# A hybrid diffusion block: full-height filter products, and adaLN products on two column tiles

## The chip, the core and the metric

The kernel runs on one core of a Trainium2 chip. The metric is the time of one execution in microseconds of the device; lower is better. Engines are named as in the profile: PE (TensorE matmuls), PEld (TensorE weight loads), DVE (VectorE), ACT (ScalarE), POOL (GpSimd) and SP (SyncE, which issues most transfers).

## The reference, cut to what matters

One layer of a diffusion backbone over 512 latent tokens and 256 context tokens of width 1024. An adaLN vector (`silu(c) @ w_mod + b_mod`, for the latent and for the context condition) gives shifts and scales; the normed and modulated tokens go through one input projection into three mixers (a gated DeltaNet, a Hyena long convolution, an RG-LRU recurrence); their gated sum is projected and added; then comes a gated ConvFFN.

The change touches two things that are computed before the first projection. The first is the Hyena filter:

```python
hid = jnp.sin(f2 * (hid @ w2 + b2))            # (512, 64)
filt = (hid @ w3).reshape(n, 2, HY_WIDTH)      # two filters of 1024 channels
filt = filt * jnp.exp(-t * deltas)[:, None, :]
```

whose Fourier spectrum multiplies the sequence later. The second is the first third of the adaLN product, the shift and scale of norm 1: a product of the two condition vectors (1024 long) with a 1024 x 2048 part of `w_mod`.

## The kernel before, in words

All matmuls that need single precision are either float32 matmuls (each shows as two LDWEIGHTS and two MATMUL records) or sums of float32r products of a high and a low part (one record each). Everything of interest is the opening stage, before the first input projection. Its order is written out by hand: the string `ORDER` is a list of steps, each a letter and a number, and every engine and SP's queue keeps its instructions in the order of that list. Steps that matter:

- `M`: load 512 KB of `w_mod` (16 of them, M0 to M15), into a ring of six 4 KB buffers; `D`: load decay factors; `x`: load 1/8 of the tokens; `s`: store a spectrum; `L`: load and split a projection weight.
- `m` (`mod_mm`, lines 378 to 383): unit u multiplies the 128 x 32 condition tile (two columns used) with both 512-column halves of buffer u, into two PSUM banks, both at partitions 0 to 31. Units 10, 11 and 13 are split first by the steps `p10`, `p11` and `P13` (`mod_split`, lines 370 to 375: one ACT copy, two subtractions on DVE or POOL) and multiplied as two float32r products.
- `a`, `A` (`filt`, line 320): filter u, eight matmuls with 256 columns. They alternate between a product of all 128 rows (the high parts of `w3` against `hid2`, which holds the high part of the hidden layer in rows 0 to 63 and the low part in rows 64 to 127) and one of 64 rows (the low part of `w3`, line 331). DVE multiplies each result by the decay (line 333), ACT and DVE or POOL split it (lines 155 and 160).
- `b`, `B` (`spectrum`): 24 products of 128 rows and 256 columns (lines 173 to 175), then DVE, ACT and POOL work on the results (lines 347 to 362).
- `q`, `Q`, `N`, `O`, `n`, `y`: sums of squares, the norm, and the scaling of the tokens by it (lines 399 to 420). `V`: split `w3` on ACT and POOL (line 455).
- `T`, `E` (`mod_T`, `mod_out`): transposes of the adaLN results out of PSUM (line 389), then scale and shift. `h` (`h_out`): modulate one eighth of the tokens on ACT, POOL and DVE (lines 437 to 439); the first input projection needs all eight.

On PE the order is: l0 m0 l1 m1 m2 a0 m3 A1 m4 m5 B0 A2 m6 m7 A3 m8 b1 b2 A4 b3 N B4 O m9 m10 m11 m12 A5 A6 a7 m13 m14 m15 b5 b6 b7, then the first projection. PSUM results of filters and spectra share four banks (`dn`).

Of the kernel before, what the change touches and what calls it, by code (L numbers as in the profile page):

```python
# [10 lines left out]
F32 = mybir.dt.float32  # L11
F32R = mybir.dt.float32r
AF = mybir.ActivationFunctionType
ALU = mybir.AluOpType
# [3 lines left out]
P = 128  # L18
D = 1024
# [3 lines left out]
KD = D // P  # L23
# [38 lines left out]
def seq(off, kb, n):  # L62
    return [off + kb * i for i in range(n)]
# [2 lines left out]
ARENA = 196  # L66


ORDER = """W l0 U0 M D x1 u1 m0 M x4 x2 M M x3 M x0 f0 V1 V0 l1 m1 m2 M f1 Q0 a0 D m3 M A1 q1 m4 m5 Q2 B0 M A2 x5 q3 M D m6 m7 q4 T0 x6 I q5 M A3 m8 b1 x7 Q6 b2 Q7 A4 b3 N K L0 M p10 s1 M p11 B4 O n4 M m9 m10 m11 m12 T1 D M s2 y7 n1 s3 M y0 P13 s4 n3 y5 n2 A5 A6 a7 M m13 m14 m15 E y6 b5 h0 h1 b6 h2 h3 s0 b7 h4 h5 L1 h6 h7 s5 s6 s7"""
FBT = (1, 4)  # L70


# [1 line left out]
def tile_block(ctx: ExitStack, tc: tile.TileContext, I: dict, out: bass.AP, dbg=None, upto=99):  # L74
    nc = tc.nc
# [7 lines left out]
    def shaped(ap, shape):  # L83
        shape = list(shape)
        if len(shape) == 2:
            return ap
        names = "abcde"[:len(shape) - 1]
        return ap.rearrange("p (%s) -> p %s" % (" ".join(names), " ".join(names)),
                            **{n: d for n, d in zip(names[1:], shape[2:])})

    def at(off, shape, dt=F32, kb=None):

        n = int(np.prod(shape[1:]))
        size = int(kb * 256) if kb else n
        assert n <= size and off * 256 + size <= ARENA * 256, (shape, off, kb)
        key = (off, size, dt)
        if key not in regions:
            regions[key] = nc.alloc_sbuf_tensor_at(f"region{len(regions)}", [P, size], dt, offset=base + int(off * 1024)).ap()
        return shaped(regions[key][0:shape[0], 0:n], shape)

    def ring(kb, offs):
        return Ring(at, kb, offs)
# [11 lines left out]
    def c1(shape, name, dt=F32):  # L114
        return sb.tile(shape, dt, tag=name, bufs=1, name=name)
# [9 lines left out]
    act = nc.scalar.activation  # L125
    stt = nc.vector.scalar_tensor_tensor
    vtt = nc.vector.tensor_tensor
    gtt = nc.gpsimd.tensor_tensor
    mmul = nc.tensor.matmul
# [5 lines left out]
    def pv(name):  # L135
        o, w = POFF[name]
        return pc[:, o:o + w]
# [14 lines left out]
    def split(raw, hi, lo, e_hi="pool", e_lo="dve"):  # L152

        if e_hi == "act":
            act(hi, raw, AF.Copy)  # L155
        elif e_hi == "pool":
            nc.gpsimd.tensor_scalar(hi, raw, 1.0, 0.0, op0=ALU.mult, op1=ALU.add)  # L157
        else:
            nc.vector.tensor_copy(hi, raw)
        (vtt if e_lo == "dve" else gtt)(lo, raw, hi.bitcast(F32), op=ALU.subtract)  # L160
# [56 lines left out]
    hid2 = at(147, [P, 512], F32R)  # L217
    kk = at(151, [P, 512])
    w3 = [at(153 + 4 * i, [P, D]) for i in range(2)]
    w3f, w3h, w3l = ([at(o_ + 4 * i, [P, D], t_) for i in range(2)] for o_, t_ in ((161, F32), (153, F32R), (161, F32R)))  # L220
# [36 lines left out]
        decs.append(decr([P, 4, 256]))  # L257
        load(decs[-1], I["c_decay"][len(decs) - 1])

    wmr, wmh, wml = ring(4, seq(28, 4, 6)), ring(4, seq(52, 4, 2)), ring(4, seq(60, 4, 2))  # L260
    FR = [int(s_[1:]) for s_ in ORDER.split() if s_[0] in "pP"]
    wms, whl = [], {}
    modps = [banks[4 + b] for b in range(4)]

    def mod_load():
# [11 lines left out]
    cc = c1([P, KD, 2], "cc")  # L277
    ccp = at(194, [P, KD, 32])
    nc.vector.memset(ccp, 0.0)
    act(cc, pv("cc").rearrange("p (k two) -> p k two", two=2), AF.Silu)  # L280
    nc.vector.tensor_copy(ccp[:, :, 0:2], cc)
    ccr = c1([P, KD, 32], "ccr", F32R)
    if FR:
        cch, cc32 = c1([P, KD, 2], "cch", F32R), at(193, [P, KD, 32])
        nc.vector.tensor_copy(cch, cc)
        nc.gpsimd.memset(cc32, 0.0)
        nc.gpsimd.tensor_copy(cc32[:, :, 0:2], cc)
        gtt(cc32[:, :, 2:4], cc, cch.bitcast(F32), op=ALU.subtract)
        nc.gpsimd.tensor_copy(ccr, cc32)
    C1, C2 = 6.28125, 0.0019353071795864769  # L290

    def rsin(x):
# [28 lines left out]
    def filt(u, e_lo="dve"):  # L321
        qr, sig = divmod(u, 2)
        cs_ = slice(qr * 256, qr * 256 + 256)
        f2 = flt[u] = fhr([P, 2, 4, 256], F32R)
        for t2_ in range(2):
            ps = dn([P, 2, 256])
            for u_ in range(2):
                tau = t2_ * 2 + u_
                ts_ = slice(tau * P, (tau + 1) * P)
                mmul(ps[:, u_], hid2[:, ts_], w3h[sig][:, cs_], start=True, stop=False)  # L330
                mmul(ps[:, u_], hid2[0:64, ts_], w3l[sig][0:64, cs_], start=False, stop=True)
            tmp = tmpr([P, 2, 256])
            vtt(tmp, ps, decs[qr][:, t2_ * 2:t2_ * 2 + 2], op=ALU.mult)
            split(tmp, f2[:, 0, t2_ * 2:t2_ * 2 + 2], f2[:, 1, t2_ * 2:t2_ * 2 + 2], "act", e_lo)
# [32 lines left out]
        for z_ in range(2):  # L367
            load(Hd[qr, :, 2 * sig + z_], spec[u][z_])

    def mod_split(u, pool=False):  # L370
        w_, wh_, wl_ = wms[u], wmh([P, 2, 512], F32R), wml([P, 2, 512], F32R)
        act(wh_, w_, AF.Copy)
        (gtt if pool else vtt)(wl_[:, 0], w_[:, 0], wh_[:, 0].bitcast(F32), op=ALU.subtract)
        gtt(wl_[:, 1], w_[:, 1], wh_[:, 1].bitcast(F32), op=ALU.subtract)
        whl[u] = wh_, wl_

    def mod_mm(u):
        hf, k = divmod(u, KD)
        parts, c_ = (whl[u], ccr) if u in whl else ((wms[u],), ccp)
        for b in range(2):  # L380
            for h_ in parts:
                mmul(modps[hf * 2 + b][0:32, :], c_[:, k, :], h_[:, b, :],
                     start=(k == 0 and h_ is parts[0]), stop=(k == KD - 1 and h_ is parts[-1]))

    modT = at(141, [P, 16, 32])

    def mod_T(b):
        for q in range(4):
            nc.vector.transpose(modT[q * 32:q * 32 + 32, 4 * b:4 * b + 4, :],
                                modps[b][0:32, :].rearrange("p (g q c) -> p g q c", g=4, q=4)[:, :, q, :])  # L390

    acc = sqr([P, NT])
    rs = at(144, [P, NT])
# [3 lines left out]
    def square(k, tt_=vtt):  # L397
        sq = acc if k == 0 else sq_r([P, NT])
        act(sq, xk[k], AF.Square)
        if k:  # L400
            tt_(acc, acc, sq, op=ALU.add)
# [16 lines left out]
    def normed(k, tt_=gtt):  # L418
        vtt(xk[k][:, 0:NX], xk[k][:, 0:NX], rs[:, 0:NX], op=ALU.mult)
        tt_(xk[k][:, NX:], xk[k][:, NX:], rs[:, NX:], op=ALU.mult)  # L420

    mod1 = c1([P, 16, 2], "mod1")
    sc1 = c1([P, 8, 2], "sc1")

    def mod_out():
        mod_T(2)
        mod_T(3)
        if FR:
            vtt(mod1, modT[:, :, 0:2], modT[:, :, 2:4], op=ALU.add)
        vtt(mod1, mod1 if FR else modT[:, :, 0:2], pv("b_mod")[:, 0:16].unsqueeze(2).to_broadcast([P, 16, 2]), op=ALU.add)  # L430
        stt(sc1, mod1[:, 8:16, :], 1.0, pv("norm1_g").unsqueeze(2).to_broadcast([P, 8, 2]), op0=ALU.add, op1=ALU.mult)

    def h_out(k):
# [19 lines left out]
    def w3_split(i, tt_):  # L453
        act(w3h[i], w3f[i], AF.Copy)
        tt_(w3l[i][0:64], w3f[i][0:64], w3h[i][0:64].bitcast(F32), op=ALU.subtract)

    def fb_load(i):
        fload(fb[:, :, 2 * i:2 * i + 2], cfw[:, :, 2 * i:2 * i + 2], wms[FBT[i]][0:1, 0, 0:1])
# [3 lines left out]
    def lx_load(g):  # L462
        wlx[g] = load_w(I["w_in"][BLK_LX + g])

    steps = {"L": lx_load, "m": mod_mm, "p": mod_split, "P": lambda u: mod_split(u, True), "Q": lambda k: square(k, gtt),
             "A": lambda u: filt(u, "pool"), "B": lambda u: spectrum(u, True), "y": lambda k: normed(k, vtt),
             "u": lambda i: w3_sum(i, vtt), "U": lambda i: w3_sum(i, gtt), "v": lambda i: w3_split(i, vtt),
             "V": lambda i: w3_split(i, gtt), "T": mod_T, "a": filt, "b": spectrum, "h": h_out, "q": square, "n": normed,
             "x": x_load, "s": spec_store, "f": fb_load, "l": layer_}
    single = {"M": mod_load, "D": dec_load, "I": lambda: load(ident, I["c_ident"]), "W": w3_load, "K": lambda: load(mask, I["c_mask"]),  # L470
              "N": norms, "O": norms_out, "E": mod_out}
    for s_ in ORDER.split():
        if s_ in single:
# [95 lines left out]
    def lru_y(g):  # L569

        w = load_w(I["w_in"][BLK_LY + g], e_lo=YLO)
        py = mm()
        project(w, [(py, hh, hl)])
        y, u = yr_([P, NL]), yr_([P, NL])
        act(u, py, AF.Square, scale=math.sqrt(0.044715))
        stt(u, u, 1.0, py, op0=ALU.add, op1=ALU.mult)
        act(u, u, AF.Sigmoid, scale=2.0 * GC)
        vtt(y, u, py, op=ALU.mult)
        return y, u
# [70 lines left out]
    for g in range(8):  # L650
# [9 lines left out]
        y, u = lru_y(g)  # L660
# [623 lines left out]
    x2 = at(28, [P, 4, D])  # L1284
    m2, m5, fg = (at(44 + 4 * i, [P, D]) for i in range(3))
# [343 lines left out]
```

## Time and profile before

| | us |
|---|---|
| median of three runs | 1701.33 |
| lowest and highest of the three | 1699.63, 1703.97 |
| the profiled execution's own time | 1699.04 |
| its span, first to last instruction | 1696.9 |

The span of a profile is counted from its first instruction; starts given below are on that count. A busy time is the time in which an engine had an instruction in work; the ends of matmuls are modelled, so what a series of matmuls costs is read from one start to the next. The granted clock is 1.00 when TensorE had its 2.4 GHz throughout a stretch and 0.50 when it had 1.2 GHz.

### The profile page before, as it was taken

Reading aid. Unit: us, or ns where it says so; the run is one execution under the profiler, and the core shown is the slowest. Engines: PE = TensorE matmul, PEld = TensorE weight load, DVE = VectorE, ACT = ScalarE, POOL = GpSimd, SP = SyncE. Lnnn points to the kernel's source line nnn. Section 1 sums busy time; section 2 is a strip of 40 time slices with the busy share of each in tenths; the row PEclk is TensorE's granted clock in tenths of the full one; section 3 lists DMA queues with packets and bytes.
Section 4 is the critical chain, followed back from the end, with each engine's and each line's share of the span. In section 5 each row is a group of like instructions: output and inputs, shape, how many; then the busy total and the mean of one; then the engine's idle time right before and its main releaser. Section 6 shows DMA issues by size and latency. Waiting matters only on the chain. (4 is left out here: it accounts for less than half of the span.)

```text
span 1696.9 us, 23679 instructions
## 1 busy us (share of the span) xinstructions
PE 1554.4 (92%) x9176; PEld 1264.1 (74%) x9176; DVE 1202.8 (71%) x1756; ACT 618.8 (36%) x1014; POOL 587.0 (35%) x407
## 2 busy tenths in 40 slices
PE   6989989889999988987899999999999999999998
PEld 1657767668787766875687777778878788888876
DVE  4677798765655999553675566777665899989873
ACT  3447878753454222231111150332222433333311
POOL 3752444433535351221333313222321234333441
PEclk7989999989999998788999999999999999999999
DMA  8522222234534332467889646322452123232331
GB/s 304 183 93 69 81 74 70 98 111 136 166 108 135 117 92 90 124 196 190 243 238 247 220 173 229 112 87 86 157 191 89 63 87 99 95 104 93 106 112 50
DMA packets 93057, 225.66 MB, mean 133 GB/s; under 512 B 9963, under 2 KB 30699, under 8 KB 92176
## 3 DMA queue, kind: packets, MB, share of 16 engines
q1 hardware_dynamic: 92112, 217.86, 40.9%
q0 software_dynamic: 832, 6.29, 0.9%
q8 instruction: 72, 1.18, 0.3%
q14 instruction: 41, 0.34, 0.1%
HBM read 190.45 MB, written 33.66 MB: 132 GB/s over the span
## 5 line engine op out<-in xcount | busy, mean ns | idle before, releaser
L173 PE MATMUL bank<-region,region 128*128 128x512 f32 (+1 forms) x2032 | 761.4, 376 | 23.8 <-DVE region L507 7.6
L175 PE MATMUL bank<-region,region 128*128 128x512 f32 (+1 forms) x2032 | 755.4, 373 | 24.6 <-DVE region L160 21.3
L174 PE MATMUL bank<-region,region 128*128 128x512 f32 (+1 forms) x2032 | 756.9, 373 | 5.0 <-DVE region L439 2.9
L173 PEld LDWEIGHTS bank<-region,region 128*128 128x128 f32 x2032 | 389.5, 192 | 101.6 <-ACT region L539 9.0
L175 PEld LDWEIGHTS bank<-region,region 128*128 128x128 f32 x2032 | 389.7, 192 | 97.7 <-DVE region L160 27.8
L174 PEld LDWEIGHTS bank<-region,region 128*128 128x128 f32 x2032 | 390.3, 192 | 69.6 <-DVE region L439 4.9
L160 DVE TENSOR_TENSOR region<-region,region 128x1024 fp32r<-128x1024 f32 (+2 forms) x241 | 269.8, 1133 | 173.0 <-ACT region L155 94.9
L155 ACT ACTIVATE region<-region 128x1024 fp32r<-128x1024 f32 (+2 forms) x209 | 178.4, 865 | 427.4 <-PE bank L174 130.0
L160 POOL TENSOR_TENSOR region<-region,region 128x1024 fp32r<-128x1024 f32 (+1 forms) x64 | 155.3, 2431 | 251.2 <-ACT region L155 210.8
L157 POOL TENSOR_SCALAR region<-region 128x1024 fp32r<-128x1024 f32 (+1 forms) x96 | 113.0, 1178 | 337.8 <-PE bank L174 151.2
L1443 DVE SCALAR_TENSOR_TENSOR region<-bank,pc,region 128x441 f32<-128x441 f32 (+2 forms) x352 | 224.8, 688 | 4.3 <-ACT region L1432 0.7
L505 DVE SCALAR_TENSOR_TENSOR region<-bank,pc,region 128x511 f32<-128x511 f32 (+1 forms) x56 | 34.1, 630 | 51.1 <-ACT region L502 47.3
L1074 DVE SCALAR_TENSOR_TENSOR region<-region,cc,region 128x1024 f32<-128x1024 f32 x28 | 42.1, 1504 | 35.9 <-DMA region<-in_w_mod_dram 35.5
L1012 POOL TENSOR_TENSOR region<-region,region 128x512 f32<-128x512 f32 x32 | 45.8, 1460 | 38.3 <-DMA region<-rowd 37.3
L502 ACT ACTIVATE region<-bank,pc 128x512 f32<-128x512 f32 (+1 forms) x40 | 23.0, 597 | 96.2 <-PE bank L175 96.2
L1455 POOL TENSOR_TENSOR region<-region,region 128x512 f32<-128x512 f32 x22 | 34.3, 1560 | 66.1 <-DVE region L1443 52.2
L1048 DVE SCALAR_TENSOR_TENSOR region<-region,egl,bank 128x128 f32<-128x128 f32 x160 | 42.3, 340 | 19.2 <-PE bank L1043 19.2
L1025 PE MATMUL bank<-region,region 128*64 128x128 f32 x608 | 38.9, 287 | 9.4 <-DVE region L1048 9.3
L1025 PEld LDWEIGHTS bank<-region,region 128*64 128x64 f32 x608 | 35.9, 145 | 14.6 <-DVE region L1048 6.3
L1037 ACT ACTIVATE region<-bank 128x512 f32<-128x512 f32 x24 | 14.3, 598 | 88.1 <-PE bank L1035 87.7
L594 ACT ACTIVATE region<-bank 128x512 f32<-128x512 f32 x32 | 18.8, 587 | 70.1 <-PE bank L175 66.0
L1035 PE MATMUL bank<-region,region 64*64 64x128 f32 x384 | 28.3, 298 | 12.7 <-DVE region L1029 6.9
(286 smaller groups left out, 1697.1 us busy)
## 6 DMA issues: line engine op xcount, KB each, us to landing
region<-in_w_in_dram SPq DMA_DIRECT2D x97, 512.0 KB, 3.6
region<-in_w_mod_dram SPq DMA_DIRECT2D x48, 512.0 KB, 6.7
region<-in_ffn_up_dram SPq DMA_DIRECT2D x44, 512.0 KB, 3.5
region<-in_w_proj_dram SPq DMA_DIRECT2D x24, 512.0 KB, 3.7
region<-in_ffn_down_dram SPq DMA_DIRECT2D x22, 512.0 KB, 3.4
gated<-region SPq DMA_DIRECT2D x32, 256.0 KB, 2.1
region<-gated SPq DMA_DIRECT2D x32, 256.0 KB, 3.5
kdd<-region SPq DMA_DIRECT2D x16, 384.0 KB, 2.8
```

The source lines that it names most:

```text
L155: act(hi, raw, AF.Copy)
L157: nc.gpsimd.tensor_scalar(hi, raw, 1.0, 0.0, op0=ALU.mult, op1=ALU.add)
L160: (vtt if e_lo == "dve" else gtt)(lo, raw, hi.bitcast(F32), op=ALU.subtract)
L173: mmul(ps, lh, rh, start=start, stop=False)
L174: mmul(ps, lh, rl, start=False, stop=False)
L175: mmul(ps, ll, rh, start=False, stop=stop)
L1012: gtt(wq[d][:, hs], KQ[hf][:, :, chs[d] - 4], eg[:, hs].unsqueeze(2).to_broadcast([P, 4, 2, 64]), op=ALU.mult)
L1025: mmul(X[hf][rcs[d], h, :], wq[d][:, hf * 4 + h, kind], S[d][:, hf * 4 + h, :], start=(kind == 0 or h == 0), stop=(kind == 0))
L1048: stt(S[d][:, h], S[d][:, h], egl[:, d, c, i, h:h + 1], p3[hf][d][:, h % 4], op0=ALU.mult, op1=ALU.add)
L1074: stt(acc, w_, cc[:, k, 0:1], acc, op0=ALU.mult, op1=ALU.add)
L1443: stt(uv[:, ro, co], pv_[:, ri, ci], w[:, a * 3 + b:a * 3 + b + 1], uv[:, ro, co], op0=ALU.mult, op1=ALU.add)
L1455: gtt(uu[0], uu[0], uu[1], op=ALU.mult)
```

## The change

The low part of `w3` gets 64 rows of zeros below it (two memsets on POOL, behind the steps `V1` and `V0`), and the second filter product uses all 128 rows. The adaLN products are all unsplit: the steps p10, p11 and P13 leave `ORDER`, with the preparation of their condition tile and one addition at the end. The second column block of each unit is written to partitions 32 to 63 of its bank, that is to another column tile of TensorE, and the transposes read it there. The ring of `w_mod` buffers has eight places instead of six. The rest of `ORDER` is as it was.

```diff
-    wmr, wmh, wml = ring(4, seq(28, 4, 6)), ring(4, seq(52, 4, 2)), ring(4, seq(60, 4, 2))
-    FR = [int(s_[1:]) for s_ in ORDER.split() if s_[0] in "pP"]
-    wms, whl = [], {}
+    wmr = ring(4, seq(28, 4, 8))
+    wms = []
...
-    ccr = c1([P, KD, 32], "ccr", F32R)
-    if FR:
...
-        nc.gpsimd.tensor_copy(ccr, cc32)
...
-                mmul(ps[:, u_], hid2[0:64, ts_], w3l[sig][0:64, cs_], start=False, stop=True)
+                mmul(ps[:, u_], hid2[:, ts_], w3l[sig][:, cs_], start=False, stop=True)
...
-    def mod_split(u, pool=False):
...
     def mod_mm(u):
         hf, k = divmod(u, KD)
-        parts, c_ = (whl[u], ccr) if u in whl else ((wms[u],), ccp)
         for b in range(2):
-            for h_ in parts:
-                mmul(modps[hf * 2 + b][0:32, :], c_[:, k, :], h_[:, b, :],
-                     start=(k == 0 and h_ is parts[0]), stop=(k == KD - 1 and h_ is parts[-1]))
+            mmul(modps[hf * 2 + b][b * 32:b * 32 + 32, :], ccp[:, k, :], wms[u][:, b, :], start=(k == 0), stop=(k == KD - 1))
...
-                                modps[b][0:32, :].rearrange("p (g q c) -> p g q c", g=4, q=4)[:, :, q, :])
+                                modps[b][b % 2 * 32:b % 2 * 32 + 32, :].rearrange("p (g q c) -> p g q c", g=4, q=4)[:, :, q, :])
...
-        if FR:
-            vtt(mod1, modT[:, :, 0:2], modT[:, :, 2:4], op=ALU.add)
-        vtt(mod1, mod1 if FR else modT[:, :, 0:2], pv("b_mod")[:, 0:16].unsqueeze(2).to_broadcast([P, 16, 2]), op=ALU.add)
+        vtt(mod1, modT[:, :, 0:2], pv("b_mod")[:, 0:16].unsqueeze(2).to_broadcast([P, 16, 2]), op=ALU.add)
...
         tt_(w3l[i][0:64], w3f[i][0:64], w3h[i][0:64].bitcast(F32), op=ALU.subtract)
+        nc.gpsimd.memset(w3l[i][64:].bitcast(F32), 0.0)
```

## Rows read from the trace of the kernel before

**Rows 1.** The core: span and mean granted clock; from the page, its busy engines.
```profile
core 0: 1696.9 us, clock 0.957
...
PE 1554.4 (92%) x9176; PEld 1264.1 (74%) x9176; DVE 1202.8 (71%) x1756; ACT 618.8 (36%) x1014; POOL 587.0 (35%) x407
```

**Rows 2.** Windows of the opening stage: length, busy time (instructions) by engine, PEclk, DMA.
```profile
25.60:41.40 15.80, 15.80 (x25) 5.99 (x26) 5.51 (x7) 4.27 (x7) 2.85 (x3) 0.50 0.67 253
41.50:67.40 25.90, 25.90 (x137) 17.40 (x136) 11.73 (x17) 11.16 (x17) 14.94 (x11) 1.00 0.48 149
67.40:87.70 20.30, 17.12 (x74) 9.54 (x72) 19.81 (x21) 5.82 (x9) 16.64 (x12) 0.87 0.67 232
87.70:98.00 10.30, 9.55 (x19) 3.72 (x20) 5.92 (x10) 3.68 (x6) 5.42 (x4) 0.60 0.00 0
```

**Rows 3.** Timeline of DVE in the opening stage.
```profile
16.50 4.62 DVE L295 TENSOR_SCALAR region<-region 128x512 f32<-128x512 f32 x1
...
72.52 3.43 DVE L373 TENSOR_TENSOR region<-region,region 128x512 fp32r<-128x512 f32 x2
...
87.72 2.47 DVE L333 TENSOR_TENSOR region<-bank,region 128x512 f32<-128x512 f32 x4
...
97.98 2.55 DVE L389 STREAM_TRANSPOSE region<-bank 32x128 f32<-32x128 f32 x8 [2.58 <-PE bank L382]
```

**Rows 4.** Timeline of POOL in the opening stage.
```profile
16.19 4.64 POOL L455 TENSOR_TENSOR region<-region,region 64x1024 fp32r<-64x1024 f32 x2
...
70.11 3.60 POOL L374 TENSOR_TENSOR region<-region,region 128x512 fp32r<-128x512 f32 x2 [1.53 <-ACT region L372]
...
102.29 11.90 POOL L438 TENSOR_SCALAR region<-region,sc,mod 128x512 f32<-128x512 f32 x12 [7.73 <-ACT region L437]
```

**Rows 5.** Timeline of PE, filter a0 to norm N: start, time, instruction, idle before.
```profile
25.59 0.58 PE L330 MATMUL bank<-region,region 128*128 128x256 f32 x1 [5.74 <-DVE region L312]
...
29.68 3.62 PE L382 MATMUL bank<-region,region 128*32 128x512 f32 x4
33.23 0.58 PE L330 MATMUL bank<-region,region 128*128 128x256 f32 x1
...
37.31 5.65 PE L382 MATMUL bank<-region,region 128*32 128x512 f32 x8
42.89 0.39 PE L173 MATMUL bank<-region,region 128*128 128x256 f32 x1
...
45.87 0.28 PE L330 MATMUL bank<-region,region 128*128 128x256 f32 x1
...
48.27 3.62 PE L382 MATMUL bank<-region,region 128*32 128x512 f32 x8
...
56.16 0.38 PE L173 MATMUL bank<-region,region 128*128 128x256 f32 x1
...
67.38 1.40 PE L407 MATMUL bank<-ones,region 128*128 128x1 f32 x12
```

**Rows 6.** Timeline of PE in a later stage, where float32 matmuls alternate between two column tiles.
```profile
802.87 1.97 PE L1025 MATMUL bank<-region,region 128*64 128x128 f32 x32
804.78 1.96 PE L1035 MATMUL bank<-region,region 64*64 64x128 f32 x32
```

**Rows 7.** Groups of POOL's instructions: busy, mean ns of one, idle before.
```profile
L841 POOL MEMSET region<- 128x1024 f32 x3 | 2.9, 952 | 10.6 <-DVE region L826 7.7 <-DVE region L819 2.9
```

**Rows 8.** Timeline of PE, filter a7 and the last adaLN units.
```profile
74.81 2.08 PE L382 MATMUL bank<-region,ccr 128*32 128x512 f32 x8
...
88.45 0.58 PE L330 MATMUL bank<-region,region 128*128 128x256 f32 x1 [3.93 <-DVE region L333]
...
92.53 1.91 PE L382 MATMUL bank<-region,ccr 128*32 128x512 f32 x4
94.38 4.43 PE L382 MATMUL bank<-region,region 128*32 128x512 f32 x8
```

**Rows 9.** Waits of SP's queue, 20 to 60 us: total, times, longest.
```profile
SPq L258 <- DVE region L333: 14.8, 1, 14.8
```

More of the change, by code (lines that the diff above doesn't have):

```diff
@@ L66 @@
 ARENA = 196
-ORDER = """W l0 U0 M D x1 u1 m0 M x4 x2 M M x3 M x0 f0 V1 V0 l1 m1 m2 M f1 Q0 a0 D m3 M A1 q1 m4 m5 Q2 B0 M A2 x5 q3 M D m6 m7 q4 T0 x6 I q5 M A3 m8 b1 x7 Q6 b2 Q7 A4 b3 N K L0 M p10 s1 M p11 B4 O n4 M m9 m10 m11 m12 T1 D M s2 y7 n1 s3 M y0 P13 s4 n3 y5 n2 A5 A6 a7 M m13 m14 m15 E y6 b5 h0 h1 b6 h2 h3 s0 b7 h4 h5 L1 h6 h7 s5 s6 s7"""
+ORDER = """W l0 U0 M D x1 u1 m0 M x4 x2 M M x3 M x0 f0 V1 V0 l1 m1 m2 M f1 Q0 a0 D m3 M A1 q1 m4 m5 Q2 B0 M A2 x5 q3 M D m6 m7 q4 T0 x6 I q5 M A3 m8 b1 x7 Q6 b2 Q7 A4 b3 N K L0 M s1 M B4 O n4 M m9 m10 m11 m12 T1 D M s2 y7 n1 s3 M y0 s4 n3 y5 n2 A5 A6 a7 M m13 m14 m15 E y6 b5 h0 h1 b6 h2 h3 s0 b7 h4 h5 L1 h6 h7 s5 s6 s7"""
 FBT = (1, 4)
@@ L281, in tile_block @@
     nc.vector.tensor_copy(ccp[:, :, 0:2], cc)
-    ccr = c1([P, KD, 32], "ccr", F32R)
-    if FR:
[L284 to L288, printed above, removed]
-        nc.gpsimd.tensor_copy(ccr, cc32)
     C1, C2 = 6.28125, 0.0019353071795864769
@@ L368, in spec_store @@
             load(Hd[qr, :, 2 * sig + z_], spec[u][z_])
-    def mod_split(u, pool=False):
[L371 to L375, printed above, removed]
     def mod_mm(u):
         hf, k = divmod(u, KD)
-        parts, c_ = (whl[u], ccr) if u in whl else ((wms[u],), ccp)
         for b in range(2):
-            for h_ in parts:
-                mmul(modps[hf * 2 + b][0:32, :], c_[:, k, :], h_[:, b, :],
-                     start=(k == 0 and h_ is parts[0]), stop=(k == KD - 1 and h_ is parts[-1]))
+            mmul(modps[hf * 2 + b][b * 32:b * 32 + 32, :], ccp[:, k, :], wms[u][:, b, :], start=(k == 0), stop=(k == KD - 1))
     modT = at(141, [P, 16, 32])
@@ L463, in lx_load @@
         wlx[g] = load_w(I["w_in"][BLK_LX + g])
-    steps = {"L": lx_load, "m": mod_mm, "p": mod_split, "P": lambda u: mod_split(u, True), "Q": lambda k: square(k, gtt),
+    steps = {"L": lx_load, "m": mod_mm, "Q": lambda k: square(k, gtt),
              "A": lambda u: filt(u, "pool"), "B": lambda u: spectrum(u, True), "y": lambda k: normed(k, vtt),
```

## The prediction

> **What bounds the kernel now.** The page gives PE 92% of the span [rows 1], so I first ask in which stage the change lies and what limits that one. Windows over the opening stage [rows 2] show PE busy without a gap from the first filter product a0 (25.6 us) to the norm N (67.4): that stretch is PE's. From there to 87.7 DVE is busy 19.8 of 20.3 us: that stretch is DVE's. Then PE has 9.6 of 10.3 us up to the adaLN transposes at 98.0 [rows 3]. Behind them POOL's 16 modulating operations run from 102.29, the first twelve of them 11.9 us back to back [rows 4]; they and the first projection do not change. So the opening is one chain: PE to N, DVE to the decay product of A5, PE to the last adaLN unit, then POOL. What the chain loses, everything behind it starts earlier by; nothing behind is tied to a fixed moment.
>
> The timeline of PE [rows 5] prices each step, from start to start:
>
> - a0, 8 matmuls: 33.23 is A1's start and 29.68 m3's, so a0 is 29.68 - 25.59 = 4.09, m3 3.55, A1 4.08, m4 and m5 together 5.58 (the clock rises inside them), all others before it at the clock 0.50 [rows 2].
> - B0, 24 matmuls of 256 columns: 45.87 - 42.89 = 2.98, 0.124 each at the full clock. A2, 8 matmuls of the same 256 columns: 48.27 - 45.87 = 2.40, 0.300 each.
> - m6 and m7: 3.62, so 1.81 for a unit, or 452 ns for each of its four records of 512 columns. What is left of 56.16 - 48.27 = 7.89 after three units (5.43) is A3: 2.46. The last 11.22 are b1, b2, A4 and b3: with A4 as A2, 8.82 for the three spectra.
>
> **The change part by part.**
>
> *128 rows.* The reader is to see that the same kind of matmul with the same columns costs 0.124 where all have 128 rows and 0.300 where 128 and 64 rows alternate. The number of rows is what differs, so I price a filter at 8 x 0.124 = 0.99 at the full clock and twice that, 1.98, at half.
>
> *Two column tiles.* In the later stage 32 float32 records of 128 columns, which alternate in pairs between partitions 0 to 63 and 64 to 127 of the output, take 804.78 - 802.87 = 1.91, or 60 ns each [rows 6]. The adaLN records, all on one tile, cost 452/4 = 113 ns for 128 columns. The ratio is 0.53: two tiles run side by side. I take it over: a unit is 0.96 at the full clock and 0.53 x 3.55 = 1.88 at half. The bound on the other side is no overlap, 1.81 and 3.55; the row in hand has 64-wide tiles and shorter streams, but the same order of records, so I take its end.
>
> A rule speaks against this. The Trainium skill ("TensorE: Matmul & The Clock Gate", Part 3, The mechanism) says that a weight load overlaps a running matmul only where the row groups differ, and here both blocks use all rows; by it a unit would keep its price, as in the first rival. The later stage, at 60 ns for a record, does not agree.
>
> *a0 to N, sum.* a0 and A1 3.97; m3, m4, m5 at the half clock 5.64; B0 2.98; A2, A3, A4 2.98; m6, m7, m8 2.88; three spectra 8.82: together 27.3 where 41.8 were, so 14.5 less. If the clock rises later and B0 runs at half, that is 3.0 more.
>
> *Memsets.* Two on POOL; three of 128 x 1024 took 952 ns each [rows 7], as long per partition, so 1.9. They stand between and behind the two splits at line 455, which ended at 16.19 + 4.64 = 20.83; a DVE operation of the hidden layer that began beside them lasted to 16.50 + 4.62 = 21.12 [rows 3, 4], and it leads to a0. If it waits for the memsets as for the splits, a0 is 1.9 later; if not, 0. I take 1.9. What leaves POOL and DVE at 4 to 5 us (the split condition tile) lay in idle time and counts nothing.
>
> *Waits that take PE's place.* DVE and POOL together are busy 17.2 + 17.8 = 35.0 us between a0 and N [rows 2]. If none of that could overlap, N could come no sooner than 35.0 after a0, 7.7 more than PE's sum; if all is hidden, 0. DVE works out of PSUM for much of it while POOL works, so I take the middle, 4. N comes 14.5 - 1.9 - 4 = 8.6 earlier, at 58.8.
>
> *N to A5's decay product (20.3).* The subtractions of p10 and p11 leave DVE: 3.43 [rows 3]. The same steps' halves on POOL, 3.60 [rows 4], and P13's two, which I price alike, leave POOL; each of those made a DVE operation beside it longer. At least 1.2 goes (two DVE operations at the 0.62 of a decay product, four of which took 2.47 [rows 3]), at most 3.4 + 3.6 = 7.0. I take 4: DVE's own row and little more, because n4 has to wait for O on PE anyway. PE's four units m9 to m12 change too, three of them from split to unsplit (two split units took 2.08 [rows 8], now 1.9); they end before DVE does and cost nothing, as long as that cover stands. A5's product comes at 87.7 - 8.6 - 4 = 75.1.
>
> *A5's product to the transposes (10.3).* Before: 0.73 to a7's start at 88.45, a7 4.08, m13 1.85, and 3.60 of m14 and m15 up to 97.98 [rows 3, 8]. After, at half clock: 0.73 + 1.98 + 3 x 1.88 = 8.4; at full 4.6, but DVE has 5.9 of its own there [rows 2]. PE idles longer before a7 than the 3.93 it did [rows 8], so nearer the half clock: 7.5, 2.8 less. One addition of 0.2 goes behind the transposes.
>
> *Loads.* The eight-place ring lets `w_mod` loads queue earlier. SP's queue stood 14.8 us before the third decay load, for A1's decay product [rows 9]; x6, x7 and M9 are behind it. A1 ends earlier now and they move with it. I count nothing: the DMA is busy 0.48 and 0.67 of the two stretches behind [rows 2]. Were that cover gone, N would wait for x7.
>
> Sum: 8.6 + 4 + 2.8 + 0.2 = 15.6. The profiled execution took 1699.0 (span 1696.9 and 2.1 around it), so 1683.4; the median of the runs is 2.3 above it: 1685.7.
>
> **The rivals.**
>
> 1. *Column tiles do not overlap.* PE's sum to N is 27.3 + 3 x 1.67 + 3 x 0.85 = 34.9, with hardly any wait left below DVE and POOL's 35.0: 5.0 earlier with the memsets. Then 4, and the last stretch is 0.73 + 1.98 + 10.65 = 13.4, 3.1 longer. With the addition it is 6.1 in all: 1695. For it: the units have 32 columns where the row in hand has 64. Against it: the 60 ns.
> 2. *The filters keep their 0.300*, because something other than the rows costs it. Sum to N: 27.3 + 2.1 + 2.1 + 3 x 1.45 = 35.8, 4.1 earlier with the memsets; then 4; the last stretch is 0.73 + 4.08 + 5.64 = 10.45, 0.2 longer: 8.1 with the addition, 1693. Against it: B0's matmuls change weights each time too, and cost 0.124.
> 3. *The clock gives the gain back, in part.* The opening has PE busy for less of its time, and the mean clock of 0.957 [rows 1] has stretches at half further on. Each microsecond of PE-bound work that falls in a further such stretch takes two. With 21 to 41 us more of them, 10 to 20 us come back: no change, about 1700.
> 4. *Slower.* The same mechanism, at the first projections, where PE comes out of the wait for POOL: a half clock that lasts there. It decides from 31 us of additional half clock on (15.6 returned); slower by 0.3% takes 41, and would be 1706. The clock was 0.957 over 1696.9 us, so 1696.9 x 0.043 x 2 = 146 us were at half; over a quarter more would be needed. In the stage's own favour: a0 to B0 streams with fewer gaps than before.
>
> **How the numbers follow.** My forecast 0.70, rival 1 0.12, rival 2 0.05, rival 3 0.08, rival 4 0.05. The time is the forecast's, 1685.7. Its terms at their good ends (no waits, free memsets, 7.0, 5.9) give 26 and 1675, at their bad ends (7.7 of waits, B0 at half, 1.2, 8.4) 5 and 1696. Not all fall on one side: 1679 to 1695 takes in most of these and both partial rivals, and leaves out the last two and the tails. A measurement of this kernel tells 0.3%, 5 us, from no change. Rivals 1 and 2 are about 6 and 8 us faster, so a little over half of the first counts as faster: faster 0.82, same 0.13, slower 0.05.
>
> **What would show it.** Eight matmuls of a filter in about 1.0 us at full clock; four records of a unit in about 0.96; N at 59 (51 to 65); DVE's decay products of A5 at 75; the transposes for `mod_out` at 82 to 83; POOL's modulation some 15 to 16 earlier; a0 at 27.5. Wrong it would be if the units stay at 1.81, if PE shows long waits for line 333 or 160 between a0 and N, or if the windows behind 121 us show a lower clock than before.

## The result, and the profile after

The changed kernel takes 1676.29 us (median of 4 runs, 1674.67 to 1683.08), the kernel before 1702.65 beside it (4 runs, 1699.63 to 1704.43). The medians differ by 26.4 us. The ratio on record is 0.9855, with an interval of 0.9823 to 0.9886; it is not the quotient of the two medians (0.9845), and by it the gain is 24.7. So the change is faster, clear of the noise. 1685.7 was forecast, with 1679 to 1695 as the range: the sign was right, the size too small, and the time lies 2.7 below the range.

The core and its engines, which answer to [rows 1]:

```profile
core 0: 1675.1 us, clock 0.959
...
PE 1529.7 (91%) x9176; PEld 1258.0 (75%) x9176; DVE 1195.7 (71%) x1752; ACT 615.7 (37%) x1011; POOL 589.3 (35%) x401
```

The profiled execution took 1676.85, 22.2 less than that of before (1699.04). How much of this comes from the opening is read off five marks: the first filter product a0, the norm N, A5's decay product, the transposes for `mod_out`, and the first DVE instruction behind the opening, which was at 121.11 before and is now at 101.25, 19.9 us sooner.

The windows between these marks, and three parts of the first, answer to [rows 2]:

```profile
26.20:54.60 28.40, 26.17 (x160) 19.95 (x161) 18.32 (x25) 13.85 (x23) 17.77 (x12) 0.87 0.76 256
54.60:70.70 16.10, 11.39 (x74) 7.66 (x73) 14.79 (x19) 3.88 (x7) 11.13 (x9) 1.00 0.85 289
70.70:78.40 7.70, 6.90 (x21) 2.77 (x21) 5.94 (x9) 3.69 (x6) 5.45 (x4) 0.56 0.14 57
26.20:30.10 3.90, 3.84 (x12) 1.97 (x12) 1.89 (x4) 0.64 (x2) 0.00 (x0) 0.51 1.06 410
30.10:46.40 16.30, 14.12 (x95) 9.78 (x93) 12.04 (x16) 8.10 (x13) 10.85 (x7) 1.00 0.77 273
46.39:50.84 4.45, 4.45 (x25) 4.45 (x26) 1.83 (x3) 3.66 (x6) 3.85 (x3) 0.62 0.27 99
```

The first three lengths are the stretches of the sum: 41.8, 20.3 and 10.3 before, 28.4, 16.1 and 7.7 now. Between 54.6 and 70.7 DVE and POOL are busy 14.8 and 11.1 us where it was 19.8 and 16.6: what the splits took is gone. The last three lines show the granted clock at 1.2 GHz (0.51) for a0 and m3; from 30.1 to 46.4 it is 2.4 GHz (1.00), and over the spectrum b2, behind a wait, it is 0.62. Before, it was 0.50 up to 41.4.

PE's timeline answers to [rows 5] and [rows 8]:

```profile
26.26 0.58 PE L321 MATMUL bank<-region,region 128*128 128x256 f32 x1 [6.22 <-DVE region L303]
...
28.26 1.92 PE L364 MATMUL bank<-region,region 128*32 128x512 f32 x4
30.11 0.39 PE L321 MATMUL bank<-region,region 128*128 128x256 f32 x1
...
31.26 1.91 PE L364 MATMUL bank<-region,region 128*32 128x512 f32 x8
...
36.07 0.28 PE L321 MATMUL bank<-region,region 128*128 128x256 f32 x1
...
37.12 1.91 PE L364 MATMUL bank<-region,region 128*32 128x512 f32 x8
...
46.39 0.36 PE L173 MATMUL bank<-region,region 128*128 128x256 f32 x1 [2.18 <-DVE region L324]
...
50.84 0.28 PE L321 MATMUL bank<-region,region 128*128 128x256 f32 x1
...
54.66 1.40 PE L388 MATMUL bank<-ones,region 128*128 128x1 f32 x12
...
60.26 3.63 PE L364 MATMUL bank<-region,region 128*32 128x512 f32 x16
63.81 0.38 PE L321 MATMUL bank<-region,region 128*128 128x256 f32 x1
...
71.50 0.58 PE L321 MATMUL bank<-region,region 128*128 128x256 f32 x1 [5.52 <-DVE region L324]
...
73.51 4.89 PE L364 MATMUL bank<-region,region 128*32 128x512 f32 x12
```

A1 takes 31.26 - 30.11 = 1.15 (4.08 before, at half the clock), A2 37.12 - 36.07 = 1.05 (2.40 before, at the full clock in both). Four adaLN units, m9 to m12, take 63.81 - 60.26 = 3.55, so 0.89 each, where m6 and m7 took 1.78 each before (48.27 to A3's start at 51.83). Between a0 and N, PE now has one long wait, 2.18 for a decay product ahead of b2. PE is no longer the stretch's bound throughout.

DVE's and POOL's timelines up to a0, and DVE's marks, answer to [rows 3] and [rows 4]:

```profile
16.71 2.35 DVE L286 TENSOR_SCALAR region<-region 128x512 f32<-128x512 f32 x1
19.09 1.14 DVE L287 TENSOR_SCALAR region<-region 128x512 f32<-128x512 f32 x1
20.26 3.43 DVE L289 SCALAR_TENSOR_TENSOR region<-region,region 128x512 f32<-128x512 f32 x2
...
70.76 3.08 DVE L324 TENSOR_TENSOR region<-bank,region 128x512 f32<-128x512 f32 x5
...
78.44 2.56 DVE L370 STREAM_TRANSPOSE region<-bank 32x128 f32<-32x128 f32 x8 [0.25 <-PE bank L364]
...
101.25 0.16 DVE L469 TENSOR_SCALAR nlam<-pc 128x16 f32<-128x16 f32 x1
```

```profile
16.41 2.35 POOL L434 TENSOR_TENSOR region<-region,region 64x1024 fp32r<-64x1024 f32 x1
18.82 1.12 POOL L435 MEMSET region<- 64x1024 f32 x1
20.02 2.39 POOL L434 TENSOR_TENSOR region<-region,region 64x1024 fp32r<-64x1024 f32 x1
22.48 0.95 POOL L435 MEMSET region<- 64x1024 f32 x1
...
82.40 11.93 POOL L417 TENSOR_SCALAR region<-region,sc,mod 128x512 f32<-128x512 f32 x12 [4.76 <-ACT region L416]
```

The memsets take 1.12 and 0.95 on POOL, near the price, but the first one lets DVE in between the splits: line 286's operation ends at 19.06, behind the first split (18.76), where the same operation lasted to 21.12 before, to the end of both [rows 3, 4]. The modulation takes its old 11.9 us and starts 19.9 sooner.

### The profile page after: what moved, and what is told of

Its sections match the earlier page's. It is cut to its first block, busy times and chain, and to the rows that moved or that the text cites. A ratio compares the mean times of both kernels' runs of the same rounds, so it can differ in the third digit from the quotient of the medians.

```text
span 1675.1 us, 23659 instructions
## 1 busy us (share of the span) xinstructions
PE 1529.7 (91%) x9176; PEld 1258.0 (75%) x9176; DVE 1195.7 (71%) x1752; ACT 615.7 (37%) x1011; POOL 589.3 (35%) x401
## 5 line engine op out<-in xcount | busy, mean ns | idle before, releaser
L992 POOL TENSOR_TENSOR region<-region,region 128x512 f32<-128x512 f32 x32 | 49.1, 1564 | 39.5 <-DMA region<-rowd 36.8
L482 ACT ACTIVATE region<-bank,pc 128x512 f32<-128x512 f32 (+1 forms) x40 | 23.1, 597 | 98.6 <-PE bank L175 98.6
L1435 POOL TENSOR_TENSOR region<-region,region 128x512 f32<-128x512 f32 x22 | 34.3, 1561 | 66.3 <-DVE region L1423 52.3
L1005 PE MATMUL bank<-region,region 128*64 128x128 f32 x608 | 42.4, 306 | 9.2 <-DVE region L1028 9.2
L1005 PEld LDWEIGHTS bank<-region,region 128*64 128x64 f32 x608 | 39.8, 157 | 14.4 <-DVE region L1028 6.4
L1137 POOL TENSOR_TENSOR region<-region,region 128x512 f32<-128x512 f32 x8 | 12.2, 1523 | 85.6 <-DVE region L1121 85.6
```

What stands on the lines that cost most here:

```text
L992: gtt(wq[d][:, hs], KQ[hf][:, :, chs[d] - 4], eg[:, hs].unsqueeze(2).to_broadcast([P, 4, 2, 64]), op=ALU.mult)
L1005: mmul(X[hf][rcs[d], h, :], wq[d][:, hf * 4 + h, kind], S[d][:, hf * 4 + h, :], start=(kind == 0 or h == 0), stop=(kind == 0))
L1435: gtt(uu[0], uu[0], uu[1], op=ALU.mult)
```

## The experiments

Theory A is the prediction's: the rows shorten PE's filters, the two tiles shorten PE's units, the unsplit units relieve DVE and POOL. Its rivals: the tiles do nothing (rival 1), the filters' price is not the rows' (rival 2), or (theory B) the relief of DVE and POOL is the whole gain. Three series were run, each beside runs of the kernel before (medians 1699.55, 1698.61 and, one run, 1697.06).

The marks of every kernel, in us from the start of its own profiled execution ("behind" is the first DVE instruction behind the opening, "gain" 121.11 less that):

| kernel | a0 | N | A5's product | transposes | behind | gain | time, ratio and interval |
|---|---|---|---|---|---|---|---|
| before | 25.59 | 67.38 | 87.72 | 97.98 | 121.11 | | |
| changed | 26.26 | 54.66 | 70.76 | 78.44 | 101.25 | 19.9 | 1676.29, 0.9855 (0.9823-0.9886) |
| e1_rows_only | 26.41 | 56.01 | 77.62 | 84.95 | 108.07 | 13.0 | 1687.74, 0.9942 (0.992-0.9963) |
| e2_tiles_only | 26.00 | 61.25 | 77.36 | 87.12 | 109.97 | 11.1 | 1692.03, 0.9945 (0.9916-0.9975) |
| e3_one_tile | 25.73 | 56.44 | 72.52 | 79.86 | 102.73 | 18.4 | 1685.83, 0.9926 (0.9899-0.9952) |
| e4_unsplit_only | 26.12 | 67.83 | 83.78 | 95.50 | 118.54 | 2.6 | 1696.9, 0.9983 (0.9956-1.001) |
| e5_changed_again | 25.95 | 54.37 | 70.47 | 77.83 | 100.64 | 20.5 | 1680.25, 0.9891 (0.9852-0.993) |
| e6_half_changes | 25.38 | 60.25 | 80.58 | 89.43 | 112.57 | 8.5 | one run, 1697.31 |
| e7_modulate_on_act | 26.52 | 53.78 | 69.99 | 77.67 | 98.58 | 22.5 | 1674.97, 0.9875 (0.9816-0.9934) |
| e8_before_again | 25.84 | 67.57 | 87.90 | 98.16 | 121.31 | -0.2 | one run, 1697.84 |
| e9_ring_six | 26.57 | 53.84 | 70.04 | 77.46 | 100.37 | 20.7 | one run, 1672.12 |
| e10_memsets_thrice | 24.92 | 54.44 | 70.64 | 77.99 | 100.87 | 20.2 | one run, 1685.93 |
| e11_tiles_again | 25.57 | 61.40 | 77.49 | 87.63 | 110.55 | 10.6 | one run, 1689.69 |

Two profiled executions of one kernel give the opening to 0.2 us (before), 0.6 (changed) and 0.6 (tiles alone). The opening's gain is therefore the finer measure of a part, though it says nothing of what lies behind the opening; whole times of one kernel scatter by more (22 runs of the kernel before in the first series lie between 1691.59 and 1710.88).

**e1_rows_only**: the kernel before, with 128 rows in the filters alone.

```diff
-                mmul(ps[:, u_], hid2[0:64, ts_], w3l[sig][0:64, cs_], start=False, stop=True)
+                mmul(ps[:, u_], hid2[:, ts_], w3l[sig][:, cs_], start=False, stop=True)
+        nc.gpsimd.memset(w3l[i][64:].bitcast(F32), 0.0)
```

> Only the filter products are changed (128 rows, zeros below, two memsets); the adaLN units stay split and on one column tile. Theory A (each change of the row count between neighbouring matmuls costs PE some 0.18 us, and PE sets the way to the norm): a filter of eight matmuls takes about 1.0 us at full clock where it took 2.4, the norm N comes 8 to 10 us sooner than at 67.4, and the kernel gains 8 to 12 us over the kernel before. Theory B (the gain of the whole change is the relief of DVE, ACT and POOL from the three splits): under 3 us. Theory C (the two column tiles alone make the gain): under 3 us.

N is 11.4 sooner than before and the opening gains 13.0. A filter's matmuls now start 0.12 apart, in its timeline of PE:

```profile
43.48 0.28 PE L331 MATMUL bank<-region,region 128*128 128x256 f32 x1
43.60 0.28 PE L330 MATMUL bank<-region,region 128*128 128x256 f32 x1
43.72 0.28 PE L331 MATMUL bank<-region,region 128*128 128x256 f32 x1
```

Rival 2 falls, and so does theory B: the splits are all still there. N to A5's product is 21.6, where it was 20.3.

**e2_tiles_only and e11_tiles_again**: the changed kernel with the filters' low product on 64 rows again, and no memsets; the same file twice.

```diff
-                mmul(ps[:, u_], hid2[:, ts_], w3l[sig][:, cs_], start=False, stop=True)
+                mmul(ps[:, u_], hid2[0:64, ts_], w3l[sig][0:64, cs_], start=False, stop=True)
-        nc.gpsimd.memset(w3l[i][64:].bitcast(F32), 0.0)
```

> Only the adaLN products are changed (unsplit, two column tiles, eight buffers); the low filter product keeps its 64 rows and there are no memsets. Theory A (two tiles run side by side): a unit takes 0.9 us at full clock and 1.8 at half where it took 1.8 and 3.55; N comes 6 to 9 us sooner, DVE's way from N to the decay product of A5 is 3 to 5 shorter, and the kernel gains 8 to 12 us. The clock stays at half as long as before in the stretch of a0 to m5, since the filters are as they were. Theory B (relief from the splits): about 5 us, all of it behind N. Theory D (the rows alone make the gain): under 4 us.

> The kernel with the two column tiles and 64-row filters once more, because the records of the granted clock were missing in the opening of its first look. If the alternating filters keep the clock down whatever the adaLN units do, the half clock lasts 10 us or more from a0 on, and a0 and A1 take 4.0 us each; if the two tiles alone lift it, A1 takes 2.4.

The opening gains 11.1 and 10.6, N comes 6.1 and 6.0 sooner, and N to A5's product is 4.2 shorter. The whole time of e2 gains 7.5, a little less than expected. The records of the granted clock are missing from the opening of e2's profile, which is why e11 was run: a0 and A1 take 4.07 and 4.08 there, so the two tiles alone did not lift the clock; more of it below.

**e3_one_tile**: the changed kernel with both column blocks on the first column tile, unsplit.

```diff
-            mmul(modps[hf * 2 + b][b * 32:b * 32 + 32, :], ccp[:, k, :], wms[u][:, b, :], start=(k == 0), stop=(k == KD - 1))
+            mmul(modps[hf * 2 + b][0:32, :], ccp[:, k, :], wms[u][:, b, :], start=(k == 0), stop=(k == KD - 1))
-                                modps[b][b % 2 * 32:b % 2 * 32 + 32, :].rearrange("p (g q c) -> p g q c", g=4, q=4)[:, :, q, :])
+                                modps[b][0:32, :].rearrange("p (g q c) -> p g q c", g=4, q=4)[:, :, q, :])
```

> The changed kernel with one thing taken back: both column blocks of a unit are written to partitions 0 to 31 again, so all units are unsplit on one column tile; the filters have 128 rows. Theory A: units take 1.8 us at full clock again; m13 to m15 cost 2.5 to 5 us more on the way to the transposes, and N comes some 5 us later than in the changed kernel: the kernel is 6 to 10 us slower than the changed one, 12 to 16 us faster than the one before. Theory D (the rows alone, with the relief from the splits): within 3 us of the changed kernel.

Two units on one tile, in its timeline of PE:

```profile
40.13 3.62 PE L364 MATMUL bank<-region,region 128*32 128x512 f32 x8
```

The next filter starts at 43.68, so a unit takes 3.55 / 2 = 1.78, against 0.89 on two tiles. The tiles overlap and rival 1's mechanism falls. By its whole time e3 came as expected: 13.7 faster than the kernel before beside it, and 5.6 to 9.5 slower than the two medians of the changed kernel (1680.25 and 1676.29, from other series). Its opening, though, lost only 1.5 us. Windows over e3, from a0 to N and from A5's product to the transposes:

```profile
25.73:56.44 30.71, 30.71 (x161) 19.96 (x161) 18.45 (x24) 13.98 (x23) 16.34 (x12) 0.90 0.68 237
...
72.52:79.86 7.34, 6.61 (x21) 2.39 (x21) 5.83 (x10) 3.68 (x6) 5.45 (x4) 1.00 0.18 71
```

Up to N, PE is busy throughout, 30.7, where the changed kernel has 26.2 and 2.2 of waits. From N to A5's product the stretch stays 16.1 in both; the dearer units lie beside DVE's work. The last stretch, with three units at the double price, was even shorter than in the changed kernel (7.3 against 7.7), because the clock was 1.00 in it and 0.56 there. So part of what the tiles save in the opening was given back by the clock. Why the whole time lost some 4 to 8 us more than the opening is not settled.

**e4_unsplit_only**: the edits of e2 and e3 together, so that only the unsplit units and the eight-place ring are left.

> The splits alone are taken out: all units are unsplit on one column tile, eight buffers, filters with 64 rows as before. Theory A: PE pays 0.8 us more for each of three units, DVE has 3.4 us less between N and A5's decay product; between 4 us faster and 1 us slower than before. Theory B (relief from the splits is the gain): 12 us or more faster.

Windows over it, from 42 us to N and from there to A5's product:

```profile
42.00:67.83 25.83, 25.83 (x136) 17.35 (x135) 11.76 (x17) 11.14 (x17) 14.94 (x11) 1.00 0.48 148
...
67.83:83.78 15.95, 15.95 (x69) 8.49 (x67) 14.24 (x19) 2.99 (x6) 9.52 (x8) 1.00 0.78 267
83.78:95.50 11.72, 11.72 (x25) 4.45 (x25) 5.45 (x10) 3.72 (x6) 5.42 (x4) 0.71 0.09 37
```

PE has no gap in any of the three. The second is 4.4 shorter than before, as in each unsplit kernel (15.95 to 16.2), but the third is 1.5 longer, and N does not move: 2.6 in all. Theory B falls a second time.

**e6_half_changes**: the kernel before, with the second column block's two products in reverse order, so that two products of 64 rows and two of 128 follow one another. The arithmetic and the number of rows stay; the changes between 128 and 64 rows are halved.

```diff
-                mmul(ps[:, u_], hid2[:, ts_], w3h[sig][:, cs_], start=True, stop=False)
-                mmul(ps[:, u_], hid2[0:64, ts_], w3l[sig][0:64, cs_], start=False, stop=True)
+                if u_ == 0:
+                    mmul(ps[:, u_], hid2[:, ts_], w3h[sig][:, cs_], start=True, stop=False)
+                mmul(ps[:, u_], hid2[0:64, ts_], w3l[sig][0:64, cs_], start=(u_ == 1), stop=(u_ == 0))
+                if u_ == 1:
+                    mmul(ps[:, u_], hid2[:, ts_], w3h[sig][:, cs_], start=False, stop=True)
```

> The kernel before, with only the order of the two products turned round in every second column block of a filter (high low low high instead of high low high low): the same matmuls with 64 and 128 rows, but the number of rows changes half as often. Theory A (each change costs some 0.18 us): a filter of eight takes about 8 x 0.124 + 4 x 0.18 = 1.7 us at full clock where it took 2.4. Theory A2 (a product of 64 rows is slow by itself, whatever stands beside it): 2.4 as before.

A filter in its timeline of PE:

```profile
40.71 0.28 PE L331 MATMUL bank<-region,region 128*128 128x256 f32 x1
40.91 0.50 PE L332 MATMUL bank<-region,region 64*128 64x256 f32 x2
41.34 0.38 PE L334 MATMUL bank<-region,region 128*128 128x256 f32 x1
41.57 0.28 PE L331 MATMUL bank<-region,region 128*128 128x256 f32 x1
...
42.20 0.38 PE L334 MATMUL bank<-region,region 128*128 128x256 f32 x1
```

The second product of the first pair, from a window inside it:

```profile
41.14 0.28 PE L332 MATMUL bank<-region,region 64*128 64x256 f32 x1
```

The next unit starts at 42.51, so eight matmuls take 1.80 (2.40 before, 1.05 for A2 in the changed kernel). Inside a filter the number of rows changes seven times before, four times here and never in the changed kernel. Three changes fewer save 0.60, so 0.20 each, and all seven 1.35, so 0.19 each. What costs is the change between row counts, not a product of 64 rows itself: two products of 64 rows start 41.14 - 40.91 = 0.23 apart, and the two of 128 rows behind them 41.57 - 41.34 = 0.23.

The weight loads show where the time goes. Between products of the same number of rows a load starts 0.12 ahead of its matmul (first line, e1; its matmul starts at 43.48); at a change it starts together with its matmul (second line, the kernel before; its matmul starts at 46.08):

```profile
43.36 0.19 PEld L331 LDWEIGHTS bank<-region,region 128*128 128x128 f32 x1
...
46.08 0.18 PEld L331 LDWEIGHTS bank<-region,region 64*128 64x128 f32 x1
```

Why the load waits at a change is not shown. The order alone gives 8.5 us of the opening, a part of it through the clock (0.78 from 25.6 to 41.4, where it was 0.50); its whole time, one run of 1697.31, is no clear gain.

**e5_changed_again and e8_before_again**: the two kernels unaltered, beside e6 and e7.

> The changed kernel again, unaltered, beside the others of this series, to see what one look more says of the clock in the opening and of the later stages. The transposes that begin mod_out came at 78.4 us in the first profile. If the opening sets the gain, they come at 77 to 81 again and the whole gain lies between 15 and 28 us; if the first profile was lucky in its clock, they come later than 83.

> The kernel before again, for one look more at the clock of its opening. In its first profile the clock fell to half shortly before a0 and rose 17 us later, inside m5. If the alternating filters keep the clock down, the half clock lasts 13 us or more from a0 on again; if that was the chance of one execution, it lasts as short as in the kernel with the filters alone changed (3.4 us) or is missing.

The openings come out again to 0.2 and 0.6 us. The whole time of the changed kernel came out 4.0 higher, with an interval that overlaps the first (0.9852 to 0.993 against 0.9823 to 0.9886).

**e7_modulate_on_act**: the changed kernel with four of POOL's sixteen modulating operations on ACT, since the stretch behind the transposes is POOL's.

```diff
-            nc.gpsimd.tensor_scalar(xt[:, n], xt[:, n], sc, sh, op0=ALU.mult, op1=ALU.add)
+            if d and k % 2:
+                act(xt[:, n], xt[:, n], AF.Identity, scale=sc, bias=sh)
+            else:
+                nc.gpsimd.tensor_scalar(xt[:, n], xt[:, n], sc, sh, op0=ALU.mult, op1=ALU.add)
```

> The changed kernel, with one thing more: in h_out the context half of every second eighth of the tokens is modulated by ACT instead of POOL (four of POOL's sixteen operations). Theory P (behind mod_out the opening is POOL's: its sixteen operations run without a gap): the first instruction of DVE behind the opening, at 101.2 us in the changed kernel, comes 3 to 5 us sooner. Rival (the first projection on PE or DVE's subtractions hold that end): under 1 us.

From the transposes to the mark behind the opening it takes 20.9, where the changed kernel takes 22.8: 1.9 less (the mark itself comes 2.7 sooner), not the 3 to 5 expected. POOL now waits for ACT's output (0.97 and 0.72 us in its timeline) where it ran without a gap, and DVE is busy for 19.6 of the 20.9. At 1674.97 it is the lowest median of the series, 5.3 below e5, with intervals that overlap (0.9816 to 0.9934 against 0.9852 to 0.993).

**e9_ring_six and e10_memsets_thrice**: the changed kernel with the old six places for adaLN weights; and with each memset done three times (the same zeros).

```diff
-    wmr = ring(4, seq(28, 4, 8))
+    wmr = ring(4, seq(28, 4, 6))
...
-        nc.gpsimd.memset(w3l[i][64:].bitcast(F32), 0.0)
+        for _ in range(3):
+            nc.gpsimd.memset(w3l[i][64:].bitcast(F32), 0.0)
```

> The changed kernel with the ring of w_mod buffers at six places as before. If the ring counts for nothing, as the prediction had it, the norm N comes at 53.5 to 55.5 us and the transposes of mod_out at 77 to 79.5, as in the two looks at the changed kernel; if earlier loads carry a part of the gain, N comes 1 us or more later.

> The changed kernel with each of the two memsets done three times, so POOL has four more of about 1 us between and behind the splits of w3. If the DVE operations of the hidden layer wait for POOL's memsets as they do for its splits, as the prediction took it, a0 starts 3 to 4 us later than at 26.0 to 26.3; if DVE works beside a memset, a0 starts within 1 us of it.

Neither moves the opening (20.7 and 20.2). With three memsets a0 starts at 24.92, sooner than with one. DVE in e10 ahead of a0, POOL's first memsets, and PE's second product of a0:

```profile
18.81 1.14 DVE L287 TENSOR_SCALAR region<-region 128x512 f32<-128x512 f32 x1
19.98 1.42 DVE L289 SCALAR_TENSOR_TENSOR region<-region,region 128x512 f32<-128x512 f32 x2
...
18.54 3.30 POOL L436 MEMSET region<- 64x1024 f32 x3
...
27.38 0.58 PE L322 MATMUL bank<-region,region 128*128 128x256 f32 x1 [1.88 <-POOL region L436]
```

Its first three memsets run from 18.54 to 21.84. The two operations of line 289 take 1.42 beside them; in the changed kernel they stand beside the second split and take 3.43. The memsets do reach PE by another way: a0's second product, the first that reads the zeros, waited 1.88 for the last of them, so a0 was done at 29.18 (28.26 in the changed kernel). N came at 54.44 all the same.

## Why the prediction fell short

The forecast missed by 9.4 us. The opening's part is 4.3. Another 2.3 the profiled execution gained beyond its opening (22.2 - 19.9), for which the sum had no term. The last 2.8 are the sum's last term: I put the median 2.3 above the profiled execution, as before, and it lies 0.6 below. The opening's part alone would have left the time inside the range, and so would the other two; it took both. That the first four runs lie outside is in part chance: the six of e5 have a median of 1680.25, inside.

**The step that failed is "a0 to N"**, as terms of the sum: N came 12.7 sooner, not 8.6. That is 4.1 of the 4.3 us that the opening (19.9) has over the 15.6. The mechanism held; three sizes were wrong.

- *The half clock of m4, m5 and A1.* I kept it up to B0, as before. It ended at 30.1. A1 took 1.15 where 1.98 stood in the sum, m4 and m5 1.84 where 3.76: 2.8 less. Against it, b2 ran slowly, 50.84 - 46.39 = 4.45 where a spectrum had 2.94: 1.5 more. Both are of this execution: in e7 and e9 A1 took 2.01 and 1.93, as forecast, and b2 2.94 and 2.95. How long the half clock lasts was in part chance.
- *The waits.* I took 4, with 7.7 as the bound, since DVE and POOL are busy 35.0 us between a0 and N and one might not overlap the other. The stretch took 28.4 with 18.3 of DVE and 17.8 of POOL in it: at least 18.3 + 17.8 - 28.4 = 7.7 of them did overlap, and PE idled 28.4 - 26.2 = 2.2. That is 1.8 less. The sum of two engines' busy times was no floor.
- *The memsets.* I made a0 1.9 later; it was 0.7 later, and in e10 it came sooner than before with 6 memsets. 1.2 less. DVE did not wait for them to their end, as it did for the splits.

Together 2.8 - 1.5 + 1.8 + 1.2 = 4.3, of which the small differences of the other terms take back 0.2. The last term counts for less than it seems, since N does not follow a0: in the five profiled executions that have both parts a0 lies between 24.92 and 26.57 and N between 53.8 and 54.7, with the latest a0 ahead of one of the earliest N.

**The other steps held.** At the full clock a filter takes 0.95 to 1.15 up to its neighbour's start (0.99 forecast) and a unit 0.89 to 0.98 (0.96). The 1.81 that I halved for it was the length of a merged row; from start to start a unit took 1.78, which changes nothing. N to A5's product is 16.1 (16.3), from there to the transposes 7.7 (7.5), and behind them little moved: 22.8 against 23.1 before. The loads and the ring count nothing (e9).

**In the opening the parts do not add.** The rows alone give 13.0, the tiles with the unsplit units 10.6 to 11.1, all together 19.9. What is missing lies between a0 and N. That stretch is 41.8 before, 35.3 and 35.8 with the tiles and unsplit units (e2, e11), 28.4 with all, and with the rows alone (e1):

```profile
26.41:56.01 29.60, 29.60 (x161) 19.41 (x161) 18.46 (x24) 13.96 (x22) 16.32 (x12) 0.94 0.68 235
```

With either part alone PE is busy throughout the stretch (e1 here; in e2 35.25 of 35.25, in e11 35.83 of 35.83): the rows shorten it by 12.2, the tiles with the unsplit units by 6.0 to 6.5. With both, in the changed kernel's profile, PE waits 2.2 for DVE and runs b2 slowly (1.5), and the gain is 13.4. These two make 3.7 of the 4.8 to 5.3 that are missing; the rest was not taken apart. Against e4 (2.6), the tiles are worth 8.0 to 8.5 with 64 rows in the filters; against e3 (18.4), 1.5 with 128 rows, and the clock has a part in that 1.5. The rows are worth more than the tiles alone in every order (13.0 first, 15.8 beside unsplit units on one tile, 8.8 to 9.3 beside two tiles). Whole times cannot settle it: the medians of e1 and e2 gain 11.8 and 7.5, 19.3 together, against 26.4 and 18.4 for the two medians of the changed kernel.

**The rest of the 26.4 is not settled.** With the opening's 19.9 in place of 15.6, the sum gives 1681.4, inside the range. The profiled execution has 1.9 us more than the opening's gain in its span, the median more still. But the same difference, span gained less opening gained, is -1.9 in e5, +5.9 in e9, +3.6 in e7, -7.5 in e10 and -8.3 in e3, with nothing altered behind the opening. Half-clock stretches that come and go make at least part of it. Windows over e3, and over the changed kernel, at the same place:

```profile
369.00:380.00 11.00, 11.00 (x42) 9.22 (x41) 2.47 (x8) 3.73 (x8) 0.00 (x0) 0.53 0.17 52
```

```profile
369.00:380.00 11.00, 11.00 (x56) 9.24 (x55) 3.26 (x5) 4.18 (x7) 2.10 (x2) 1.00 0.22 58
```

PE is busy throughout in both; the clock is 0.53 in the one and 1.00 in the other, and 56 records pass where 42 did. e2 and e10 have such a stretch there too (0.85 and 0.63 in the same window). In the kernel before, too, the two longest of the 22 runs (1710.53 and 1710.88) have the lowest mean clock, 0.951. This is rival 3's mechanism, but it comes with single executions, and it was not seen to follow the change: the mean clock is 0.951 to 0.962 in the runs of the kernel before and 0.955 to 0.961 in the ten of the changed one, and from the mark behind the opening on it is 0.96 in the profiles of both. The second series' 18.4 us (1698.61 - 1680.25) is as good a figure for the change as the first's 26.4, and the opening's 19.9 and 20.5 lie between them. Rival 4 was not seen.

## What to carry to other kernels

Where matmuls of 128 and of 64 rows alternate, price the change between them: zeros under the short operand (13.0 us of this opening), or just an order with fewer changes (8.5), can be worth more than the work that they add. Of two parts that relieve the same engine, price the second against the stretch as the first leaves it, its clock included, and look for the engine that is next. Do not take the sum of two engines' busy times as a floor, nor the old clock for a stretch whose work has changed.

## What was not expected of the hardware

*The clock under alternating rows.* From a0 up to 41.4 us PE is busy without a gap in the kernels with 64 and 128 rows in turn and in those with 128 rows throughout (what a window below lacks of 15.80 lies ahead of a0; only e10 has a gap, of 1.9, inside). Yet the granted clock stayed at 1.2 GHz for all or most of it in the first, and the others reach 2.4 GHz sooner. How much of the time PE is busy, by which rivals 3 and 4 went, does not tell the two apart here. The mean granted clock from 25.6 to 41.4 us was 0.50 in the kernel before [rows 2], in e8 and in e4, and 0.56 in e11; with half the changes (e6) 0.78; with 128 rows 0.89 (e1), 0.81 (e3), 0.86, 0.87 and 0.79 (changed, e5, e10). In e2, e7 and e9 the records of the clock are missing up to 32 us or later, and no mean can be given; the matmuls of a0 and A1 stand 0.21 apart in e7 and e9, as at half the clock. Windows over e11, and over the changed kernel:

```profile
25.60:41.40 15.80, 15.80 (x45) 7.55 (x46) 5.51 (x7) 4.54 (x8) 4.37 (x3) 0.56 0.79 287
```

```profile
25.60:41.40 15.80, 15.14 (x82) 9.10 (x83) 9.60 (x12) 9.22 (x14) 7.42 (x5) 0.86 0.99 358
```

That the alternation is the cause was not tried apart from the filters' other work, which also takes longer with it; the ten openings with clock records agree with it.

*Memsets and DVE.* Line 289's operations, with two inputs, took 1.71 us each on average where a split ran on POOL, and 0.71 beside memsets. Line 287's, with one input, took 1.14 beside a memset, no more in e10 with three memsets than with one. The Trainium skill ("SBUF — State Buffer", Who interferes with whom) says that a DVE instruction with two inputs from SBUF contends with a GpSimd instruction that reads SBUF, not with one that only writes it; line 289's rows agree. One input alone does not keep an operation clear of a split, though: line 286's has one, and it lasted to 19.06 beside the split that ended at 18.76.
